# Features-first inputs and outputs, and a final norm that sums squares by products with ones

## The chip, the cores and the metric

One core of one Trainium2 chip runs the whole program. The metric is the device time of one execution in microseconds (us); lower is better. The engines are TensorE (PE in the profile, with its weight loads as PEld), VectorE (DVE), ScalarE (ACT), GpSimd (POOL) and SyncE (SP), which issues the DMAs of this kernel. Each engine runs its own instructions in order and waits on semaphores for the others.

## The reference

One layer of a streaming encoder, on a prompt of 2048 tokens and a sample of 32 (T = 2080), with 1024 features, in float32. Differential attention (group A, 4 heads of two 64-wide maps) and band attention (group B, 8 heads of 64) share one input projection and one output projection; then an MLP of 4096 with squared ReLU, a gated input embedding `p`, and a final norm:

```python
hp = hp + merge(oa, ob, subln_g[i], out_norm_b[i], w_out[i], lam_init)
hp = ffn_ple(hp, p_prompt[i], g_mlp[i], w_up[i], w_down[i], w_ple_gate[i], w_ple_proj[i])
...
y_prompt = rmsnorm(hp, g_final)

def ffn_ple(h, p, g_mlp, w_up, w_down, w_ple_gate, w_ple_proj):
    c = rmsnorm(h, g_mlp)
    h = h + jnp.square(jax.nn.relu(c @ w_up)) @ w_down
    return h + jax.nn.sigmoid(h @ w_ple_gate) * (p @ w_ple_proj)
```

Returned are `y` for prompt and sample, and the new keys and values of both groups.

## The kernel before

Features lie on the 128 partitions, tokens on the free axis, in four blocks of 512 tokens (the last has 544, worked in two slices of 272). Each product in float32 precision is made of three: both operands are split into a rounded high part and the rest (`split`: ACT makes the high part, POOL or DVE the low one), and `mm3` (lines 216 to 218) adds high x high, high x low and low x high in PSUM. Weights come through `wunit`: a load into `wr`, then the split into `wh` and `wl` (`piece` in the later stages).

The tensors in memory have tokens first, so the kernel turns blocks with TensorE, by transposes against the identity `ident`:

- `prep` (line 360) loads a tile of 128 tokens, sums its squares on ACT, turns it (`xp`, line 380), makes the activations `aH` and `aL` from PSUM with the gain, and writes the turned tile to the scratch `xT`, from which `outproj` later reads the residual `hd`.
- `knat` in `proj` turns the new keys back to tokens first (`ktp`, lines 516 and 525) for the outputs `ka_p`, `kb_p` and so on; `caches` turns the cached keys (`ctp`).
- `prep_p` turns the embedding input (`ppt`, line 907) and writes its split to the scratch `pS`, from which `gate` reads `pT`.
- `final` (line 1387) turns the finished `h` back (`yp`, line 1403), sums squares on ACT (`junk`), makes the reciprocal root for each token, multiplies with the root and the gain on DVE (line 1432) and writes rows of `y`. For block 3 the first half of the features is turned while the last gate products run (`phased`), the second half after them.

The stages follow each other: projections and attention of groups A and B, output projection `outproj`, then for each block the MLP (`mlp` for blocks 0 and 1, `mlp7` for 2 and 3), the gate and the final norm. `weave` interleaves two generators: the final of block 0 is emitted beside the MLP of block 2, that of block 2 beside the MLP of block 3, that of block 1 ahead of the output projection of block 2, and that of block 3 beside its own gate. `mlp7` computes the up products with seven instead of eight block products, with sums of weights (`s`, `wr`, lines 1255 to 1258) and of products (`u`, `r`, line 1228) on DVE and POOL; `h<-h,dps` (line 1217) adds the down products. The order on each engine is set by the tile framework's scheduler, from the order of emission and its own timeline; all DMAs go through SP's queue in that order. PSUM pools in the last part are `mm` (two banks) and `md` (six).

## Time and profile before

| | us |
|---|---|
| median of 3 runs | 3105.26 |
| lowest and highest | 3100.71, 3106.78 |
| the profiled execution | 3106.68 |
| its span in the trace | 3104.9 |
| PE busy | 2990.2 |
| POOL busy | 1852.7 |
| DVE busy | 1826.0 |
| ACT busy | 1776.4 |

In rows of groups (line, engine, operation, output<-inputs, shapes, count) the first number after the bar is the group's busy time in us, the second the mean of one in ns; after the second bar stands the idle time of the engine ahead of them and what ended it. Rows of a stretch give its bounds, its length, busy time (and count) of PE, PEld, DVE, ACT and POOL, then the granted clock, the share of the DMA engines and GB/s. Rows of a timeline give start, length, engine, line, operation and count. Rows of waits read: who waited, on whom, us in all, times, longest. A row of DMA issues gives count, KB of each and the median us from issue to landing.

### The profile page before, as it was taken

How to read it: one execution, taken by the hardware profiler on the slowest of the kernel's cores; microseconds unless marked ns; L12 is line 12 of the kernel's file. 1: busy time of each engine (PE TensorE's matmuls, PEld its weight loads, DVE VectorE, ACT ScalarE, POOL GpSimd, SP SyncE). 2: the span in 40 equal slices, each digit the busy share in tenths (PEclk: the TensorE clock that was granted, in tenths of full speed). 3: DMA queues.
4: the chain of work that ended last, by engine and by line, in shares of the span. 5: the costliest groups of instructions: out<-in, count | busy, mean ns of one | idle time of the engine just before them, and what ended most of it. 6: DMA issues, size and time to landing. Idle time of an engine off the chain costs nothing. (4 is left out here: it accounts for less than half of the span.)

```text
span 3104.9 us, 51763 instructions
## 1 busy us (share of the span) xinstructions
PE 2990.2 (96%) x17801; PEld 2637.0 (85%) x17801; DVE 1826.0 (59%) x4404; ACT 1776.4 (57%) x3434; POOL 1852.7 (60%) x2512
## 2 busy tenths in 40 slices
PE   8999989999899999999999999999899999999998
PEld 7788879899777888878888888878788887999998
DVE  6157565564565455456666656635667885576663
ACT  6256565765666666556556556554655555554545
POOL 2456746413446544556655555677878888767674
PEclk9999999999999999999999999999999999999999
DMA  9798776976877554555655454348434446333231
GB/s 283 258 263 247 224 218 187 280 221 186 247 230 226 159 155 136 154 157 167 196 152 140 124 145 139 123 150 260 155 116 130 146 158 226 118 109 102 90 117 57
DMA packets 523279, 539.19 MB, mean 174 GB/s; under 512 B 38749, under 2 KB 401569, under 8 KB 523017
## 3 DMA queue, kind: packets, MB, share of 16 engines
q1 hardware_dynamic: 523016, 535.89, 57.5%
q8 instruction: 141, 2.31, 0.3%
q14 instruction: 122, 0.99, 0.1%
HBM read 421.97 MB, written 117.75 MB: 174 GB/s over the span
## 5 line engine op out<-in xcount | busy, mean ns | idle before, releaser
L176 POOL TENSOR_TENSOR wl<-wr,wh 128x256 fp32r<-128x256 f32 x648 | 478.9, 771 | 317.8 <-ACT wh L181 277.9
L181 ACT ACTIVATE piece<-wr 128x512 fp32r<-128x512 f32 x406 | 245.4, 624 | 265.0 <-PE ups L217 111.2
L176 POOL TENSOR_TENSOR piece<-wr,piece 128x256 fp32r<-128x256 f32 x404 | 327.5, 836 | 104.6 <-ACT piece L181 85.7
L181 ACT ACTIVATE wh<-wr 128x1024 fp32r<-128x1024 f32 x228 | 240.4, 1055 | 188.1 <-PE ups L217 46.8
L166 POOL TENSOR_TENSOR wl<-wr,wh 128x256 fp32r<-128x256 f32 x264 | 201.9, 797 | 188.1 <-ACT wh L181 185.3
L216 PE MATMUL dps<-uh,piece 128*128 128x272 f32 (+1 forms) x768 | 246.3, 324 | 6.2 <-DVE h L1217 2.5
L166 POOL TENSOR_TENSOR piece<-wr,piece 128x256 fp32r<-128x256 f32 x280 | 235.1, 871 | 26.7 <-ACT piece L181 25.5
L218 PE MATMUL dps<-uh,piece 128*128 128x272 f32 (+1 forms) x768 | 246.9, 324 | 1.8 <-POOL piece L166 1.6
L217 PE MATMUL dps<-ul,piece 128*128 128x272 f32 (+1 forms) x768 | 247.3, 323 | 0.2 <-DVE ul L187 0.2
L216 PE MATMUL ups<-cs,piece 128*128 128x256 f32 (+1 forms) x864 | 245.8, 285 | 0.9 <-DVE r L1228 0.8
L217 PE MATMUL ups<-cs,piece 128*128 128x256 f32 (+1 forms) x864 | 245.7, 285 | 0.0
L218 PE MATMUL ups<-cs,piece 128*128 128x256 f32 (+1 forms) x864 | 245.5, 284 | 0.0
L216 PE MATMUL qps<-aH,wh 128*128 128x512 f32 (+1 forms) x640 | 227.9, 357 | 1.1 <-DVE ql L488 1.1
L217 PE MATMUL qps<-aL,wh 128*128 128x512 f32 (+1 forms) x640 | 228.0, 356 | 0.0
L218 PE MATMUL qps<-aH,wl 128*128 128x512 f32 (+1 forms) x640 | 227.6, 356 | 0.0
L1217 DVE TENSOR_TENSOR h<-h,dps 128x272 f32<-128x272 f32 (+1 forms) x384 | 188.9, 514 | 52.6 <-PE dps L218 51.7
L1169 DVE TENSOR_TENSOR h<-h,dps 128x512 f32<-128x512 f32 x256 | 173.3, 682 | 69.0 <-PE dps L218 67.4
L665 ACT ACTIVATE e<-e,nm 128x128 f32<-128x128 f32 (+16 forms) x136 | 157.2, 1156 | 94.9 <-DVE nm L663 92.9
L216 PE MATMUL dps<-uh,wh 128*128 128x512 f32 x512 | 207.0, 404 | 1.8 <-DVE h L1169 1.8
L216 PE MATMUL ups<-cH,wh 128*128 128x512 f32 x512 | 202.8, 397 | 1.9 <-ACT cH L181 1.9
L217 PE MATMUL ups<-cL,wh 128*128 128x512 f32 x512 | 202.5, 396 | 1.8 <-POOL cL L166 1.2
L218 PE MATMUL ups<-cH,wl 128*128 128x512 f32 x512 | 202.7, 396 | 0.0
(311 smaller groups left out, 9369.8 us busy)
## 6 DMA issues: line engine op xcount, KB each, us to landing
wr<-w_up SPq DMA_DIRECT2D x128, 512.0 KB, 4.0
wr<-w_down SPq DMA_DIRECT2D x128, 512.0 KB, 3.9
wr<-w_in SPq DMA_DIRECT2D x74, 512.0 KB, 5.5
q<-qS SPq DMA_DIRECT2D x128, 256.0 KB, 5.2
v<-vSa SPq DMA_DIRECT2D x64, 512.0 KB, 4.8
ka<-kS SPq DMA_DIRECT2D x32, 512.0 KB, 6.8
wr<-w_out SPq DMA_DIRECT2D x32, 512.0 KB, 4.6
wr<-w_ple_gate SPq DMA_DIRECT2D x32, 512.0 KB, 4.2
```

Of the source, the lines that this page charges most:

```text
L166: nc.gpsimd.tensor_tensor(out[:, sl], a[:, sl], b[:, sl], op=op)
L176: nc.gpsimd.tensor_tensor(out[:, sl], a[:, sl], b[:, sl], op=op)
L181: nc.scalar.activation(hi, raw, AF.Copy)
L216: nc.tensor.matmul(ps, lh, rh, start=start and i == 0, stop=False)
L217: nc.tensor.matmul(ps, lh, rl, start=False, stop=False)
L218: nc.tensor.matmul(ps, ll, rh, start=False, stop=stop and i == n - 1)
L665: nc.scalar.activation(row, row, AF.Exp, bias=nmx, accum_out=z[:nr, m : m + 1])
L1169: nc.vector.tensor_tensor(hv, hv, ps, op=ALU.add)
L1217: nc.vector.tensor_tensor(hv, hv, ps, op=ALU.add)
```

## The change

The host code hands `x` and `p` over a second time or only in features-first form (`x_t` and `p_t`, shape 128 x 8 x 2080 and 128 x 2 x 2080, made by `columns`), the cached keys turned (`ck_t`) and the gains as columns; `y_t` and the new keys (`ka_pt` and so on) leave features first, and numpy turns them after the launch. In the kernel:

- `prep` loads each tile twice: features first from `x_t`, multiplied with the gain on DVE and split, and tokens first from `x_prompt` for the squares alone. The scratch `xT` is gone; `outproj` reads `x_t`. The weights of the first value units get buffers of their own (`wr0`).
- `proj` writes the new keys from `kr` directly; `knat`, `prep_p` and the scratch `pS` are gone; a new `ptile` loads `p_t` and splits it at the gate.
- `final` stays features first: squares on ACT, their sum over the eight feature tiles on DVE and POOL, a split, two products with `ones` (`yss`) that sum over the partitions and spread the result, the root on ACT and DVE, and the multiplication of `h` in place, whence `y_t` is written.

```diff
@@ prep
-            x = pp.tile([P, D], F32, tag="x", name="x")
-            self.dma(x[:n], self.xsrc(t0, n))
+            xt = pp.tile([P, 8, P], F32, tag="xt", name="xt")
+            self.dma(xt[:, :, :n], self.xT[:, :, t0 : t0 + n])
...
+            x = pp.tile([P, D], F32, tag="x", name="x")
+            self.dma(x[:n], self.xsrc(t0, n))
+            m = 2 if b == 0 and i == 0 else 1
+            for k in range(0, 8, 8 // m):
+                ks = slice(k, k + 8 // m)
+                xg = xt[:, ks, :n]
+                g = self.g_attn[:, ks].unsqueeze(2).broadcast_to([P, 8 // m, n])
+                nc.vector.tensor_tensor(xg, xg, g, op=ALU.mult)
+                self.split(aH[:, ks, c0 : c0 + n], aL[:, ks, c0 : c0 + n], xg, "act", "dve")
             st = pp.tile([P, 1], F32, tag="st", name="st")
-            for h in range(2):
-                xp = mm.tile([P, 4, P], F32, tag=tag, name="xp")
-                for k in range(4):
-                    kk = 4 * h + k
-                    nc.tensor.transpose(xp[:, k, :n], x[:n, kk * P : kk * P + P], self.ident[:n, :n])
...
-            self.dma(self.xT[:, :, t0 : t0 + n], xt[:, :, :n])
+            nc.scalar.activation(x[:n], x[:n], AF.Square, accum_out=st[:n])
@@ proj
+                    if grp == 0 or b == 3:
+                        t0 = 512 * b if grp == 0 else 0
+                        self.dma(ko_p[P * g : P * g + P, t0 : t0 + 512], raw[:, :512])
+                    if b == 3:
+                        self.dma(ko_s[P * g : P * g + P], raw[:, 512 : 512 + SS])
                     yield
-                    def knat(b=b, g=g, raw=raw):
...
@@ caches
-            self.dma(kn, ck)
-            tps = tp.tile([P, 4, P], F32, tag="mm", name="ctp")
-            for g in range(4):
-                nc.tensor.transpose(tps[:, g], kn[:, P * g : P * g + P], self.ident)
+            tf = sg.tile([P, BLK], F32, tag="kr", bufs=2, name="ckr")[:, :512]
+            self.dma(tf, ck)
@@ gate
+    def ptile(self, b, up, wk):
+        n, t0 = BN[b], 512 * b
+        pT = [[up.tile([P, BLK], F32R, tag="u", name="pT") for _ in range(2)] for _ in range(2)]
+        for k in range(2):
+            raw = (
+                up.tile([P, up.aw], F32, tag="u", name="praw") if wk is None
+                else wk.tile([P, BLK], F32, tag="tmp", bufs=self.nt, name="praw")
+            )[:, :n]
+            self.dma(raw, self.pT[:, k, t0 : t0 + n])
+            self.split(pT[0][k][:, :n], pT[1][k][:, :n], raw, "act", "dve")
+        return pT
@@ final
-    def final(self, b, h, up, fk, mm, md=None):
...
+    def final(self, b, h, wk, mm):
+        nc = self.nc
+        n, t0 = BN[b], 512 * b
+        end = b == 3
+        sq = wk.tile([P, BLK], F32, tag="acc", bufs=2, name="sqy")[:, :n]
+        for k in range(8):
+            tmp = sq if k == 0 else wk.tile([P, BLK], F32, tag="tmp", bufs=self.nt, name="ysq")[:, :n]
+            for s0, sn in SUBS[b] if k == 7 else [(0, n)]:
+                sub = slice(s0, s0 + sn)
+                hv, tv, sv = h[:, k, sub], tmp[:, sub], sq[:, sub]
+                nc.scalar.activation(tv, hv, AF.Square)
+                if end and k < 7:
+                    nc.scalar.activation(hv, hv, AF.Copy, scale=self.g_final[:, k : k + 1])
+                if k > 0:
+                    if end or k % 2:
+                        nc.vector.tensor_tensor(sv, sv, tv, op=ALU.add)
+                    else:
+                        self.pool_tt(sv, sv, tv, ALU.add)
+            if end or k % 2:
+                yield
+        sh = wk.tile([P, BLK], F32R, tag="sh", bufs=1, name="sh")
+        sl = wk.tile([P, BLK], F32R, tag="sl", bufs=1, name="sl")
+        r = wk.tile([P, BLK], F32, tag="r", bufs=2, name="ry")
+        for s0, sn in SUBS[b]:
+            sub = slice(s0, s0 + sn)
+            v, y = sq[:, sub], r[:, sub]
+            self.split(sh[:, sub], sl[:, sub], v, "act", "dve")
+            ss = mm.tile([P, 512], F32, tag="mm", name="yss")[:, :sn]
+            nc.tensor.matmul(ss, self.ones, sh[:, sub], start=True, stop=False)
+            nc.tensor.matmul(ss, self.ones, sl[:, sub], start=False, stop=True)
+            nc.scalar.activation(v, ss, AF.Copy, scale=1.0 / D, bias=EPS)
+            nc.scalar.activation(y, v, AF.Ln)
+            nc.scalar.activation(y, y, AF.Exp, scale=-0.5)
+            nc.vector.scalar_tensor_tensor(v, v, -0.5, y, op0=ALU.mult, op1=ALU.mult)
+            nc.vector.tensor_tensor(v, v, y, op=ALU.mult)
+            nc.vector.scalar_tensor_tensor(y, v, 1.5, y, op0=ALU.add, op1=ALU.mult)
+            hv = h[:, 7, sub]
+            nc.vector.scalar_tensor_tensor(hv, hv, self.g_final[:, 7:8], y, op0=ALU.mult, op1=ALU.mult)
+            for k in range(6, -1, -1):
+                hv = h[:, k, sub]
+                if not end:
+                    nc.vector.scalar_tensor_tensor(hv, hv, self.g_final[:, k : k + 1], y, op0=ALU.mult, op1=ALU.mult)
+                elif k in (5, 6):
+                    self.pool_tt(hv, hv, y, ALU.mult)
                 else:
+                    nc.vector.tensor_tensor(hv, hv, y, op=ALU.mult)
+                if k % 4 == 0:
+                    self.dma(self.a["y_t"][:, k : k + 4, t0 + s0 : t0 + s0 + sn], h[:, k : k + 4, sub])
+        yield
```

The order on three engines' places follows. SP's queue at the start of the program, before (`x` is a token tile, `wr` a weight unit of the values):

```order
L157 DMA x<-x_prompt 128x1024
L157 DMA g_attn_s<-g_attn 128x8x1
L157 DMA wr<-w_in 128x4x256 x2
L157 DMA x<-x_prompt 128x1024
L157 DMA g_mlp_s<-g_mlp 128x8x1
L157 DMA g_b_s<-out_norm_b 128x4x1
L157 DMA g_sub_s<-subln_g 128x1
```

and now:

```order
L157 DMA xt<-x_t 128x8x128
L157 DMA g_attn_s<-g_attn 128x8
L157 DMA x<-x_prompt 128x1024
L157 DMA wr_142<-w_in 128x4x256
L157 DMA wr_151<-w_in 128x4x256
L157 DMA xt<-x_t 128x8x128
L157 DMA x<-x_prompt 128x1024
L157 DMA wr_178<-w_in 128x4x256
L157 DMA wr_187<-w_in 128x4x256
```

Two tiles of 512 KB now stand ahead of the first weight unit instead of one, and the small gains other than `g_attn` come behind the second pair of weights.

DVE beside the MLP of block 2, where the final of block 0 is woven in, before (`r` and `u` are sums of up products, `dps` down products, `wr` and `s` weight sums, `yn` a turned tile of `y`):

```order
L1448 TENSOR_TENSOR fst<-fst 128x1
L227 TENSOR_TENSOR rsv<-rsv,rsy 128x1
L228 TENSOR_TENSOR rsv<-rsv,rsy 128x1
L229 TENSOR_SCALAR rsv<-rsv 128x1
L231 TENSOR_TENSOR rsy<-rsy,rsv 128x1
L1432 SCALAR_TENSOR_TENSOR yn<-yn,rsy,gf 128x512 x2
L1217 TENSOR_TENSOR h<-h,dps 128x512
L1228 TENSOR_TENSOR r_26112<-t_26114,ups 128x256
```

and now (`sqy` is the sum of squares, `ry` the root):

```order
L1169 TENSOR_TENSOR r_26334<-t_26336,ups 128x256
L1369 SCALAR_TENSOR_TENSOR sqy<-sqy,ry 128x512
L1197 TENSOR_TENSOR s_26568<-wr 128x512
L1370 TENSOR_TENSOR sqy<-sqy,ry 128x512
L1169 TENSOR_TENSOR u_26365<-t_26336,ups 128x256
L1371 SCALAR_TENSOR_TENSOR ry<-sqy,ry 128x512
L1158 TENSOR_TENSOR h<-h,dps 128x512
L1373 SCALAR_TENSOR_TENSOR h<-h,g_final_s,ry 128x512
L1377 SCALAR_TENSOR_TENSOR h<-h,g_final_s,ry 128x512 x7
L1158 TENSOR_TENSOR h<-h,dps 128x512
L1198 TENSOR_TENSOR wr<-s_26568,wr 128x4x128
L1169 TENSOR_TENSOR u_26423<-u_26365,ups 128x256
```

Before, two multiplications for a token tile stood between the MLP's operations, four times in the block; now eight feature tiles are multiplied in one run. The same run stands in the MLP of block 3.

DVE at the end of the program, before (`fss` sums the squares' halves, `yo` is the second half of the features):

```order
L1384 TENSOR_TENSOR h<-h,sig 128x272
L1439 TENSOR_TENSOR fss<-fsa 128x5
L227 TENSOR_TENSOR rsv<-rsv,rsy 128x5
L228 TENSOR_TENSOR rsv<-rsv,rsy 128x5
L229 TENSOR_SCALAR rsv<-rsv 128x5
L231 TENSOR_TENSOR rsy<-rsy,rsv 128x5
L1432 SCALAR_TENSOR_TENSOR yo<-yp,rsy,gf 128x512 x4
L1432 SCALAR_TENSOR_TENSOR yo<-yp,rsy,gf 32x512
```

and now, up to the first of the two slices of 272 (the second repeats the last five rows):

```order
L1313 SCALAR_TENSOR_TENSOR sig<-gps,sig 128x272
L1351 TENSOR_TENSOR sqy<-sqy,ysq 128x272
L1328 TENSOR_TENSOR sig<-sig,pps 128x272
L187 TENSOR_TENSOR sl<-sqy,sh 128x272
L1331 TENSOR_TENSOR h<-h,sig 128x272
L1351 TENSOR_TENSOR sqy<-sqy,ysq 128x272
L187 TENSOR_TENSOR sl<-sqy,sh 128x272
L1369 SCALAR_TENSOR_TENSOR sqy<-sqy,ry 128x272
L1370 TENSOR_TENSOR sqy<-sqy,ry 128x272
L1371 SCALAR_TENSOR_TENSOR ry<-sqy,ry 128x272
L1373 SCALAR_TENSOR_TENSOR h<-h,g_final_s,ry 128x272
L1381 TENSOR_TENSOR h<-h,ry 128x272 x5
```

The root is now a row of tokens that is worked out on all partitions, once for each slice, and DVE does the six multiplications of a slice behind it; POOL does the other two.

More of the change, by code (lines that the diff above doesn't have):

```diff
@@ L190, in wunit @@
         nc = self.nc
-        raw = self.rawp.tile([P] + shape, F32, bufs=2, name="wr")
+        if pool is None:
+            raw = self.rawp.tile([P] + shape, F32, bufs=2, name="wr")
+        else:
+            raw = pool.tile([P] + shape, F32, tag="wr0", bufs=4, name="wr0")
         self.dma(raw, src)
@@ L481, in proj @@
                         )
-                        while late:
-                            late.pop(0)()
                         h_, l_ = hi[:, s0 : s0 + n], lo[:, s0 : s0 + n]
@@ L1665, in run, with columns @@
             g = self.gate(3, h, up, cs, md)
-            f = self.final(3, h, up, fk, mm, md)
-            for _ in range(5):
-                next(g)
-            for _ in range(3):
-                next(g)
-                next(f, None)
-                next(f, None)
-            drain(f)
+            f = self.final(3, h, wk, mm)
+            weave(g, f, 1)
 OUTS = {
-    "y_prompt": (1, SP, D),
-    "y_sample": (1, SS, D),
-    "ka_p": (SP, 512),
+    "y_t": (P, 8, T),
+    "ka_pt": (512, SP),
     "va_p": (SP, 512),
-    "kb_p": (512, 512),
+    "kb_pt": (512, 512),
     "vb_p": (512, 512),
-    "ka_s": (SS, 512),
+    "ka_st": (512, SS),
     "va_s": (SS, 512),
-    "kb_s": (SS, 512),
+    "kb_st": (512, SS),
     "vb_s": (SS, 512),
 }
+def columns(*parts):
+    t = np.concatenate(parts).T
+    return np.ascontiguousarray(t.reshape(-1, P, T).transpose(1, 0, 2))
 def kernel(**inputs):
     arrays = {k: np.ascontiguousarray(v) for k, v in inputs.items()}
-    for n in ("cache_a_k", "cache_a_v", "cache_b_k", "cache_b_v"):
+    for n in ("cache_a_v", "cache_b_v"):
         arrays[n] = arrays[n].reshape(PAST, 512)
+    ck = [arrays.pop(n).reshape(PAST, 4, P) for n in ("cache_a_k", "cache_b_k")]
+    arrays["ck_t"] = np.ascontiguousarray(np.stack(ck).transpose(0, 3, 2, 1)).reshape(2, P, 512)
+    arrays["x_t"] = columns(arrays["x_prompt"][0], arrays["x_sample"][0])
+    arrays["p_t"] = columns(arrays.pop("p_prompt")[0, 0], arrays.pop("p_sample")[0, 0])
+    for n in ("g_attn", "g_mlp", "out_norm_b", "subln_g", "g_final"):
+        arrays[n] = np.ascontiguousarray(arrays[n].reshape(-1, P).T)
     arrays["onehot_a"], arrays["onehot_b"] = onehots()
```

196 lines of the change are left out of this document (36 added, 160 removed).

## The prediction

> **What bounds the kernel now.** I read the page first (busy time of each engine, the 40 slices), then busy time by stretch, then the groups by line and shape, the waits, and last the two ends of the timeline.
>
> ```profile
> PE 2990.2 (96%) x17801; PEld 2637.0 (85%) x17801; DVE 1826.0 (59%) x4404; ACT 1776.4 (57%) x3434; POOL 1852.7 (60%) x2512
> PE   8999989999899999999999999999899999999998
> PEclk9999999999999999999999999999999999999999
> ```
>
> ```profile
> 80.00:100.00 20.00, 20.00 (x94) 15.50 (x93) 3.18 (x5) 2.29 (x3) 4.26 (x6) 1.00 0.78 238
> 2800.00:3000.00 200.00, 200.00 (x1601) 200.00 (x1600) 127.99 (x260) 98.45 (x170) 138.81 (x178) 1.00 0.30 96
> ```
>
> TensorE (PE) is busy 2990 of 3104.9 us, at a full granted clock, and idle for 114.7 us in all. No other engine reaches 61% (PEld is PE's own weight loads). In the two stretches it has no idle time: 94 products of 512 columns in 20 us are one each 0.213 us. So a PE instruction that goes away is worth its pitch, if what feeds PE can follow.
>
> The profiled execution took 3106.68 us, 1.8 us more than its span; the median of the three runs is 3105.26. I sum changes on the span and take them off the median.
>
> **The transposes that go.** The program loses five kinds of PE transposes against the identity: `xp` (17 token tiles x 8 = 136), `yp` (136), `ktp` (88), `ppt` (34), `ctp` (8), 402 in all. The four largest groups hold 368 of them:
>
> ```profile
> L380 PE MATMUL xp<-ident,x 128*128 128x128 f32 x128 | 20.7, 293 | 6.2 <-DMA x<-x_prompt 4.4 <-DVE kr L493 1.1 <-ACT vraw L434 0.5
> L1403 PE MATMUL yp<-ident,h 128*128 128x128 f32 x128 | 17.4, 274 | 3.8 <-ACT junk L1413 2.8 <-DVE h L1384 1.0
> L516 PE MATMUL ktp<-ident,kr 128*128 128x128 f32 x80 | 12.7, 273 | 1.8 <-ACT kn L518 1.8
> L907 PE MATMUL ppt<-ident,pn 128*128 128x128 f32 x32 | 4.9, 274 | 0.3 <-DVE ppl L911 0.3
> ```
>
> ```profile
> 2716.30 0.87 PE yp L1403 x8
> 3088.79 1.76 PE yp L1403 x16
> ```
>
> The mean of 274 ns is from start to modelled end and overlaps the next instruction. The chain of waits gives what PE is held for: 8 in 0.87 us and 16 in 1.76 us, 0.109 us each. That makes 402 x 0.109 = 43.8 us. The upper bound is the groups' busy time, 20.7 + 17.4 + 12.7 + 4.9 = 55.7 us for 368, so 60.8 us for 402: it counts each batch's pipeline end, which the following product mostly covers. I take the pitch.
>
> Not all of it is on the path. The first 16 `xp` fall where PE waits for weights anyway (below), 16 x 0.109 = 1.7 us. The last 24 `yp` come after the last gate product and belong to the tail, 2.6 us. That leaves 39.5 us.
>
> Waits that stand in front of transposes go as well: 1.1 + 0.5 (`xp`), 2.8 (`yp`), 1.8 (`ktp`), 6.2 us; the 0.3 of `ppt` I leave out, the 4.4 is the start and the 1.0 the end. The next product would find part of the same lateness (the PSUM bank of the evicting engine); I take half, 3.1 us (bounds 0 and 6.2).
>
> **What is added on PE.** Three blocks' `yss` products with ones, 6 x 0.213 = 1.3 us (the last block's four are in the tail). They stand in the order after a finished output tile, so a late sum of squares would hold PE there; the three sit beside products that do not need them, and I add nothing.
>
> **The start.** First PE products of the program, before:
>
> ```profile
> 4.41 1.94 PE L380 MATMUL xp<-ident,x 128*128 128x128 f32 x8 [4.41 <-DMA x<-x_prompt]
> 7.76 1.06 ACT L181 ACTIVATE wh<-wr 128x1024 fp32r<-128x1024 f32 x1 [1.73 <-DMA wr<-w_in]
> 8.87 0.58 PE L216 MATMUL vps<-wh,aH 128*128 128x256 f32 x1 [2.52 <-ACT wh L181]
> 8.90 5.54 POOL L176 TENSOR_TENSOR wl<-wr,wh 128x256 fp32r<-128x256 f32 x8 [7.41 <-ACT rsy L226]
> 11.34 1.91 PE L380 MATMUL xp<-ident,x 128*128 128x128 f32 x8
> 0.00:20.00 20.00, 12.16 (x64) 10.80 (x65) 10.13 (x38) 13.58 (x39) 6.47 (x15) 1.00 0.91 257
> ```
>
> PE's first real product waited for ScalarE's cast of the first weight unit, which had waited for that unit's load; POOL's eight low halves (5.54 us) then pace the next ones, and the second eight transposes fill that gap. Now a features-first tile and a token tile (512 KB each) come ahead of the weights instead of one token tile: 512 KB at that stretch's 257 GB/s is 2.0 us more. Against it, the gain vector now comes as 128 runs of 32 bytes in place of 1024 elements of 4, and the split of a tile takes three wide operations in two halves instead of eight narrow ones behind transposes. I take +1 us (bounds -1 and +3).
>
> Later loads change little: the token tiles are still read for their squares, `x_t` is read where `xT` was written (both 512-byte runs, 512 KB a tile), `pS` and its reading back go away. Nothing more is counted for them.
>
> **The final norm in the MLP.** Its vector work moves from pairs of operations per token tile to one run per block, as the order in the section on the change shows: seven multiplications that follow each other directly, eight with the one ahead. They stand in VectorE's queue (DVE) in front of the MLP's bank evictions `h<-h,dps`, the weight sums `wr` and the products `u`.
>
> ```profile
> L1432 DVE SCALAR_TENSOR_TENSOR yn<-yn,rsy,gf 128x512 f32<-128x512 f32 x24 | 24.9, 1078 | 0.4
> L1432 DVE SCALAR_TENSOR_TENSOR yo<-yp,rsy,gf 128x512 f32<-128x512 f32 x4 | 2.7, 745 | 0.1
> L1411 DVE COPY yn<-yp 128x512 f32<-128x512 f32 x24 | 15.7, 679 | 4.9 <-PE yp L1403 4.9
> PE dps L216 <- DVE h L1217: 2.5, 2, 1.8
> PE ups L216 <- DVE r L1228: 0.8, 1, 0.8
> ```
>
> Eight at 1.08 us hold DVE for 8.6 us. PE goes on in that time as long as it has banks: two in one pool and six in the other, and an output tile of six 512-column products takes 6 x 0.213 = 1.3 us, so eight banks are some 10 us. Before, two copies (1.4 us), two multiplications (2.2 us) and five small operations stood together too, and PE lost at most 1.8 us at a time to a late `h`. I take 1 us for each of the two finals that run beside an MLP, +2 us (bounds 0 and 17.2, the whole of both runs).
>
> The Trainium skill, "SBUF — State Buffer", in its account of the port pair that DVE and GpSimd share, says that a DVE operation with two SBUF inputs and a GpSimd operation that reads SBUF exclude each other for a whole instruction. The trace is in line with it: with both inputs in SBUF, in a stretch where POOL works, the multiplication takes 1078 ns, and 745 ns with one input in PSUM. The change puts more such pairs together, so by this rule the upper bound is nearer than by the banks; it is the second rival.
>
> The final of block 1 runs beside the output projection of block 2, where POOL is the nearer limit:
>
> ```profile
> 2080.00:2100.00 20.00, 18.93 (x91) 15.13 (x92) 9.94 (x16) 9.27 (x26) 14.03 (x20) 1.00 0.50 148
> 2200.00:2220.00 20.00, 14.92 (x56) 10.88 (x54) 14.55 (x18) 11.96 (x23) 18.27 (x21) 0.91 0.47 159
> L176 POOL TENSOR_TENSOR wl<-wr,wh 128x256 fp32r<-128x256 f32 x648 | 478.9, 771 | 317.8 <-ACT wh L181 277.9
> ```
>
> Six added sums of squares at 0.77 us (4.6 us) join a POOL that is 70 to 91% busy there. I take half of that block's 32 transposes as not gained, 32 x 0.109 / 2 = +1.7 us (bounds 0 and 4.6).
>
> **The tail.** After the last gate product:
>
> ```profile
> 3088.15 0.40 ACT L1362 ACTIVATE sig<-gps 128x272 f32<-128x272 f32 x1 [1.43 <-PE gps L218]
> 3088.58 0.43 ACT L1363 ACTIVATE sig<-sig 128x272 f32<-128x272 f32 x1
> 3088.63 2.46 PE L1403 MATMUL yp<-ident,h 128*32 128x128 f32 x21
> 3091.61 0.44 DVE L1384 TENSOR_TENSOR h<-h,sig 128x272 f32<-128x272 f32 x1
> 3092.11 0.55 PE L1403 MATMUL yp<-ident,h 128*128 128x128 f32 x3 [1.02 <-DVE h L1384]
> 3101.76 0.49 SPq L157 DMA_DIRECT2D y_sample<-yo  x1
> wr<-w_up SPq DMA_DIRECT2D x128, 512.0 KB, 4.0
> y_prompt<-yn SPq DMA_DIRECT2D x28, 256.0 KB, 2.1
> ```
>
> Before, from the last gate's first ScalarE step (ACT) at 3088.15 to the end are 16.75 us. Now, with a step of 272 columns at 0.46 us on ACT and 0.47 on DVE, gaps in: three ACT steps (1.4), the minimum on DVE (0.5), exponential on ACT, product, the low half of the first slice and the last add to `h` on DVE (0.47 + 3 x 0.47), square on ACT and add on DVE (0.46 + 0.47): 4.7 us. Then three steps on ACT until the first slice's exponential is done (1.4), and 2 x 9 operations on DVE, three for the root and six multiplications for each slice (18 x 0.47 = 8.5): 14.6 us. The last output of 544 KB lands 4.0 us after its issue if it goes like the 512 KB loads: 18.6 us, +1.8, say +2 (bounds: 0 with a landing as of `y_prompt`, +5 if POOL's four multiplications slow DVE's by 1078/745 and the landing is late).
>
> **The sum.** -39.5 - 3.1 + 1.3 + 1 + 2 + 1.7 + 2 = -34.6 us. From 3105.26: **3071 us**.
>
> **The rivals.**
> *Transposes cost more than their pitch* (their batches also break the stream): 60.8 in place of 43.8, on the 362 of 402 that count another 15.3 us, and all 6.2 us of waits: -34.6 - 15.3 - 3.1 = -53, 3052 us. For it speaks the busy time, against it that eight transposes between products hold PE 0.87 us.
> *DVE's runs reach PE:* both runs of eight in full, 17.2 in place of 2 us: -19.4, 3086 us. For it: behind them in DVE's queue stand evictions and weight sums. Against it: eight banks.
> *Slower: the output DMAs hold up the weights.* SP issues in order, and the two `y_t` of a final wait for DVE's run while the next `w_up` and `w_down` stand behind them.
>
> ```profile
> SPq L157 <- DVE yn L1432: 40.5, 19, 5.5
> ```
>
> If PE runs dry of weights for the run, the landing and the first low half (8.6 + 4.0 + 0.8 = 13.4 us) at each of three finals, that is 40 us, and +4 us in all, with the two DVE us already in it: 3109 us. It decides from 34.6 / 3 = 11.5 us a place. Against it: SP waited on `yn` 19 times, up to 5.5 us, and no wait of PE's comes from there.
> *The freed time is not used:* the waits of other engines (114.7 us of idle PE now) grow by what PE gains, and the time stays within 0.2%, about 6 us, which is what a measurement of this kernel can tell from none: 3104 us.
>
> **How the numbers follow.** Forecast 0.60, dearer transposes 0.15, DVE's runs 0.14, slower 0.06, not used 0.05. Faster by over 0.2%: 0.60 + 0.15 + 0.14 = 0.89; same 0.05; slower 0.06. The likeliest case's own range, from its bounds, is 3058 to 3084. The range takes in the first two rivals with their margins, 3042 to 3094, and leaves out the last two and some of the edges.
>
> **What would show it.** Right: no transpose group but `rp`, `tpp` and `tpb`; PE's instructions fewer by 392; busy PE lower by some 43 us and idle about the same 115 us; the first product at 9 to 11 us; 18 to 19 us from the last gate's first ACT step to the end. Wrong: idle PE up by 10 us or more, with waits for `h`, `r` or `piece` at the two runs of multiplications (second rival) or for loads behind `y_t` (third); or busy PE lower by about 60 us (first).

## The result, and the profile after

The changed kernel takes 3085.89 us (median of 4 runs, 3081.23 to 3090.34), the kernel before on the same chip 3102.99 us: a ratio of 0.9943, 95% interval 0.9926 to 0.9961. Run again on another chip it came to 3090.20 us, 0.9958 (0.9944 to 0.9973). By the medians it is faster by 17 and by 14 us, where the forecast was 34.6. The profiled execution has a span of 3088.5 us, 16.4 under the 3104.9 of before. Its totals, and the digits of PE's busy share and granted clock in 40 slices:

```profile
PE 2965.4 (96%) x17409; PEld 2609.3 (84%) x17409; DVE 1809.8 (59%) x4221; ACT 1751.3 (57%) x3234; POOL 1902.4 (62%) x2533
PE   6999999999899999999999999999899999999997
PEclk9999999999799999999999999999999999999999
```

392 PE instructions are gone, as the prediction counted, but busy time fell by 24.8 us instead of some 43, and idle time rose from 114.7 to 123.1. The first slice and the eleventh are the thin ones. Busy time by stretch says more, first of the kernel before:

```profile
0.00:100.00 100.00, 89.51 (x585) 78.46 (x586) 51.13 (x164) 50.01 (x140) 26.19 (x43) 1.00 0.89 275
100.00:500.00 400.00, 377.39 (x2175) 327.06 (x2174) 218.53 (x640) 226.07 (x498) 243.44 (x353) 0.98 0.79 236
500.00:1000.00 500.00, 470.96 (x2995) 422.83 (x2994) 268.34 (x885) 316.15 (x662) 209.94 (x323) 0.98 0.79 230
2000.00:3000.00 1000.00, 972.53 (x6271) 885.25 (x6270) 658.43 (x1117) 522.37 (x998) 762.01 (x933) 0.99 0.45 145
```

The same stretches of the changed kernel:

```profile
0.00:100.00 100.00, 75.51 (x473) 66.77 (x474) 49.74 (x128) 52.22 (x123) 28.55 (x37) 0.93 0.88 276
100.00:500.00 400.00, 391.29 (x2338) 344.06 (x2337) 215.17 (x564) 211.10 (x403) 275.42 (x380) 1.00 0.79 236
500.00:1000.00 500.00, 464.75 (x2756) 409.55 (x2755) 261.61 (x883) 311.75 (x647) 204.80 (x321) 0.94 0.77 224
2000.00:3000.00 1000.00, 971.83 (x6242) 885.87 (x6240) 651.24 (x1056) 524.39 (x949) 790.28 (x953) 0.99 0.44 143
```

PE does less in the first 100 us (idle 24.5 instead of 10.5), more from 100 to 500 (8.7 instead of 22.6), and less again from 500 to 1000, at a lower clock.

To put a time on each stretch I made a ledger from the start times of PE's products. Both kernels stream the same 6,162,592 columns through PE, once the transposes that go and the products with ones of the new final norm are left out. The *lead* of a kernel at a time t of the kernel before is how much earlier it has streamed as many columns. It counts the columns of any product, so work that is drawn forward raises it for a while. The forecast's own sum, laid out in the same way (76 of the 402 transposes stand in the first 100 us, then 134 to 500 us, 38 to 780, 18 to 1000, none to 2000, 96 to 3000, 40 behind; each other term at its place), stands beside it:

```
lead in us at        100    500    780   1000   1300   1400   2000   3000    end
forecast's terms     5.6   21.9   26.0   28.0   28.0   28.0   28.0   34.9   34.6
the change          -8.4   31.6   36.9   17.3   17.4   17.5   17.5   19.3   16.4
the change again   -10.9   29.3   39.5   20.2   20.4   19.7   16.2   20.1   16.5
```

Three places differ: the start (14 us under the forecast, made good by 500 us), 780 to 1000 us (20 us lost, where 2 should have been won), and all from 2000 us on (nothing won of 6.6).

**The start.** Waits of PE in the first 60 us, before (one row) and then after the change (two rows):

```profile
PE vps L216 <- ACT vraw L434: 1.0, 1, 1.0
PE vps L219 <- ACT vraw L429: 12.8, 4, 5.4
PE vps L219 <- ACT wh L181: 10.0, 1, 10.0
```

ScalarE in that stretch of the changed kernel (timeline: start, length, line, operation, idle time before it):

```profile
33.74 1.06 ACT L385 ACTIVATE x<-x 128x1024 f32<-128x1024 f32 x1 [0.85 <-DMA x<-x_prompt]
35.26 1.04 ACT L385 ACTIVATE x<-x 128x1024 f32<-128x1024 f32 x1
37.01 0.46 ACT L429 ACTIVATE vraw<-vps,rcol 128x256 f32<-128x256 f32 x1
49.19 1.06 ACT L385 ACTIVATE x<-x 128x1024 f32<-128x1024 f32 x1 [2.42 <-DMA x<-x_prompt]
50.82 1.06 ACT L385 ACTIVATE x<-x 128x1024 f32<-128x1024 f32 x1
52.76 0.47 ACT L429 ACTIVATE vraw<-vps,rcol 128x256 f32<-128x256 f32 x1
```

Twice, two squares of token tiles stand in ACT's queue in front of an eviction of the V products; the first of each pair waits for its load, and PE's next product waits for the eviction (5.3 us before 37.5, 5.4 before 53.3). One tile of each pair isn't even the start's own: the square no longer needs block 2's activation buffers, so the program's order lets block 2's token tiles run ahead into the first 70 us, where the DMA engines are busy for 97% of the time. The loads issued in that time (the start has eight tiles of each kind):

```profile
x<-x_prompt SPq DMA_DIRECT2D x13, 512.0 KB, 6.6
xt<-x_t SPq DMA_DIRECT2D x9, 512.0 KB, 7.9
```

**780 to 1000 us.** When the input projections are through, the output projection is the next work that PE can put between attention B's products. The rows below are the last projection products and the first output-projection products (first and last start at the end of the numbers), of before and then of the change:

```profile
L217 PE MATMUL qps<-aL,wh x320: 283/289/475, 529.3 to 827.4; 128*128 128x272 f32 x128, 128*128 128x512 f32 x32
L216 PE MATMUL ops<-oact,wh x128: 387/389/776, 850.1 to 980.6; 128*128 128x512 f32 x128
```

```profile
L221 PE MATMUL qps<-aH,wl x313: 282/289/476, 500.8 to 778.1; 128*128 128x272 f32 x125, 128*128 128x512 f32 x32
L219 PE MATMUL ops<-oact,wh x128: 387/389/776, 828.8 to 960.1; 128*128 128x512 f32 x128
```

The projections end 49 us earlier, the output projection begins only 21 us earlier. Between them PE has attention B alone: 22.6 us before, 50.7 us now. These are the groups of that gap in the changed kernel and then its stretch; and of the gap before the score products and the stretch:

```profile
L800 PE MATMUL sb<-kbt,q 128*128 128x320 f32 x48 | 14.7, 444 | 6.6 <-DVE stb L803 6.6
L852 PE MATMUL ob<-pb,vbt 128*128 128x512 f32 (+1 forms) x36 | 14.4, 526 | 3.7 <-DVE pb L831 3.7
L822 PE MATMUL tpb<-ident,eb 128*128 128x128 f32 x58 | 13.4, 362 | 2.5 <-DVE pb L831 2.4
778.00:828.00 50.00, 37.46 (x144) 29.11 (x143) 28.31 (x106) 33.15 (x69) 6.78 (x15) 0.66 0.70 198
```

```profile
L831 PE MATMUL sb<-kbt,q 128*128 128x320 f32 x24 | 5.8, 362 | 3.7 <-DVE stb L834 3.7
828.00:850.00 22.00, 16.21 (x85) 11.45 (x84) 14.12 (x55) 15.99 (x35) 4.34 (x8) 1.00 0.92 271
```

48 score products `sb` of attention B's heads stand in that gap; before it was 24. This is the order that the scheduler wrote: counted in the two traces, 176 score products start ahead of the last projection product now, and 204 did before. The place of the transposes was filled with projections, and not with attention's heads, whose steps on DVE and ACT follow each other. At 780 us, with as many columns streamed, the changed kernel has started 42 projection products more and 16 score products fewer; at 1000 us the counts are level but for 2 and 4. So a part of the 36.9 us at 780 us is work drawn forward, and behind it the heads' chain sets the pace alone.

### The profile page after: what moved, and what is told of

It reads as the page before. It is cut to its first block, busy times and chain, and to the rows that moved or that the text cites. A ratio compares the mean times of both kernels' runs of the same rounds, so it can differ in the third digit from the quotient of the medians.

```text
span 3088.5 us, 50476 instructions
## 1 busy us (share of the span) xinstructions
PE 2965.4 (96%) x17409; PEld 2609.3 (84%) x17409; DVE 1809.8 (59%) x4221; ACT 1751.3 (57%) x3234; POOL 1902.4 (62%) x2533
## 5 line engine op out<-in xcount | busy, mean ns | idle before, releaser
L176 POOL TENSOR_TENSOR wl<-wr,wh 128x256 fp32r<-128x256 f32 x648 | 496.0, 797 | 261.0 <-ACT wh L181 218.7
L166 POOL TENSOR_TENSOR wl<-wr,wh 128x256 fp32r<-128x256 f32 x264 | 198.4, 783 | 202.1 <-ACT wh L181 201.9
L220 PE MATMUL dps<-ul,wh 128*128 128x512 f32 x512 | 202.7, 396 | 0.0
```

The lines of the kernel that those rows point to most:

```text
L166: nc.gpsimd.tensor_tensor(out[:, sl], a[:, sl], b[:, sl], op=op)
L176: nc.gpsimd.tensor_tensor(out[:, sl], a[:, sl], b[:, sl], op=op)
L220: nc.tensor.matmul(ps, lh, rl, start=False, stop=False)
```

## The experiments

Each run is compared with the kernel before on its own chip. The ledger of all of them, with the ratio:

```
lead in us at        100    500    780   1000   1300   1400   2000   3000    end   ratio (95% interval)
late token tiles    -3.2   23.8   31.2    9.1   10.2    6.0    7.8   11.7    8.4   0.9970 (0.9955 to 0.9985)
no statistics       -0.1   40.7   46.2   27.1   27.8   25.6   24.8   29.8   27.7   0.9920 (0.9895 to 0.9945)
old start           -3.9   35.6   39.7   17.3   18.0   17.6   16.1   24.4   23.0   0.9919 (0.9895 to 0.9944)
no multiplications  -9.5   30.9   40.5   17.5   18.2   15.3   15.7   28.1   22.6   0.9952 (0.9932 to 0.9972)
first tile held     -3.7   29.2   35.1   11.5   12.4   10.3   10.0   16.8   13.7   0.9957 (0.9944 to 0.9969)
old final          -10.4   28.1   33.1   16.8   19.5   19.5   19.5   17.1   16.7   0.9938 (0.9923 to 0.9953)
old start, held      0.4   29.9   36.8   17.0   17.1   16.9   14.5   23.1   21.0   0.9939 (0.9926 to 0.9953)
norm later          -9.6   26.6   34.9   26.3   28.8   13.4    8.7   10.8    7.4   0.9969 (0.9957 to 0.9980)
before, norm later  -0.2    2.5   -1.8   -2.3   -1.0   -1.7   -2.0   -1.5   -1.4   1.0020 (1.0007 to 1.0032)
mixed                2.7   40.6   50.0   41.0   43.6   28.6   29.9   34.2   32.3   0.9905 (0.9887 to 0.9923)
mixed, q first       0.9   37.8   44.7   36.4   38.1   23.3   23.0   21.7   20.3   0.9935 (0.9919 to 0.9950)
```

Nine of the traces keep the change's order around 800 us: the change's two and the first seven kernels of this table. In all nine, 44 or 48 score products stand between projections and output projection, that gap is 45.7 to 52.4 us long, and 16 to 24 us of lead go between 780 and 1000 us, whether 31.2 or 46.2 us come in. So the place takes about a fixed amount; it does not bring every kernel to one level.

### Block 2's token tiles held back by a buffer

```diff
-            x = pp.tile([P, D], F32, tag="x", name="x")
-            self.dma(x[:n], self.xsrc(t0, n))
+            if b < 2:
+                x = pp.tile([P, D], F32, tag="x", name="x")
+                self.dma(x[:n], self.xsrc(t0, n))
...
+            if b > 1:
+                x = pp.tile([P, 8, P], F32, tag="xt", name="x").rearrange("p a b -> p (a b)")
+                self.dma(x[:n], self.xsrc(t0, n))
             st = pp.tile([P, 1], F32, tag="st", name="st")
             nc.scalar.activation(x[:n], x[:n], AF.Square, accum_out=st[:n])
```

> Blocks 2 and 3 only: the token tile of the statistics is loaded into the features-first tile's own buffer, after its split, so neither its load nor its square can run ahead of block 2's activations; the start's own tiles are as in the change. Theory 1 (token tiles of block 2 run ahead into the start, take load time there and stand with their squares in ScalarE's queue in front of the V evictions): TensorE's idle time in the first 100 us falls from 24.5 to 10 to 14 us, waits of V products for vraw in the first 60 us from 12.8 to under 3 us, the granted clock in 30 to 60 us is 1.00 again, and the time is 3069 to 3076 us, 0.989 to 0.991 of the kernel before. Theory 2 (the new preparation of blocks 0 and 1 itself costs it: two tiles to load and wide steps on ScalarE and VectorE for each): 3083 to 3088 us, idle time in the first 100 us over 20 us. Theory 3 (the gain is lost later, in attention at a lower clock): idle time may fall at the start, the time stays 3080 to 3088 us.

3095.03 us, 0.9970. The start is better as theory 1 said, but only by a third of what it asked: 20.2 us idle in the first 100, 7.1 us of waits for `vraw`. And the time is worse than the change's: none of the three theories has it there. The ledger shows where: beside the change, 8 us of lead are missing at 500 us and 6 at 780. I put that down to the serial buffer, which makes block 2's preparation late; no run isolates it. Theory 1 explains a part of the start and nothing of the time.

### No statistics at all

```diff
+        nc.vector.memset(self.rcol, 1.0)
...
-            x = pp.tile([P, D], F32, tag="x", name="x")
-            self.dma(x[:n], self.xsrc(t0, n))
...
-            st = pp.tile([P, 1], F32, tag="st", name="st")
-            nc.scalar.activation(x[:n], x[:n], AF.Square, accum_out=st[:n])
             r = self.rcol[:n, 4 * b + i : 4 * b + i + 1]
-            self.rsqrt(pp, st[:n], 1, 1.0 / D, EPS, nc.vector, "r1", n, out=r)
```

> Leaves out the tokens' statistics in all blocks: no token tile, square or root, every token's factor is one. Theory 1: what this saves over the run with late token tiles is small, 0 to 4 us, so 3066 to 3074 us. Theory 2: the price of the start's token tiles shows, 3060 to 3070 us here while the run with late token tiles stays above 3083. Theory 3: 3078 to 3086 us.

3078.87 us, 0.9920: in theory 3's range, and above those of the other two. Without token tiles the start loses 8 to 11 us less than in the change, and this lead lives: 46.2 us at 780. Yet 19 us go between 780 and 1000 here too, over a gap of 49.3 us between projections and output projection; what is left at 1000 us, 27.1, is still 7 to 10 us above the change's two executions.

### The start as before

```diff
-                gen = (y for b in HALVES[0] for y in self.prep(b, acts, pp, ring, "s", first if b == 0 else None))
+                gen = (y for b in HALVES[0] for y in self.prep_old(b, acts, pp, ring, "s", first if b == 0 else None))
```

> The preparation of blocks 0 and 1 as before (one token tile, transposes, and the write of the transposed copy, to a scratch array that nothing reads); blocks 2 and 3 and all the rest as in the change. Theory 1: block 2's token tiles can still run ahead, so the start stays disturbed: idle time of TensorE in the first 100 us 14 to 25 us, 3080 to 3090 us. Theory 2: the start is as before, idle time some 11 us, 3072 to 3078 us (the sum's 3071 plus 48 transposes of 0.109 us that are back, less the 1 us of the start). Theory 3: as theory 2 at the start, the time 3084 to 3092 us.

3078.37 us, 0.9919: at theory 2's upper edge, with idle time of 15.7 us, which is theory 1's. By the idle time both causes are at work at the start. But at 780 us the lead (39.7) is that of the change run again (39.5): the better start had been evened out by then, and the 7 us that this run is ahead at the end came after 2000 us.

### No multiplications in two finals

```diff
+            if b not in (0, 2):
-            nc.vector.scalar_tensor_tensor(hv, hv, self.g_final[:, 7:8], y, op0=ALU.mult, op1=ALU.mult)
+                nc.vector.scalar_tensor_tensor(hv, hv, self.g_final[:, 7:8], y, op0=ALU.mult, op1=ALU.mult)
```

(the other seven in the same way)

> Leaves out the eight multiplications of the final norm in blocks 0 and 2, the two finals beside an MLP; their sums, products with ones and roots stay. If the runs of multiplications cost the 2 us that the forecast gave them or less, 3083 to 3087 us. If they reach TensorE in full (the second rival of the prediction), 3068 to 3074 us.

3087.97 us, 0.9952: no faster than the change. The interval leaves out the second rival of the prediction, VectorE's runs reaching TensorE in full, whose 3068 us to 3074 us would be a ratio of 0.988 to 0.990. Whether the runs cost the 2 us of the forecast or some more stays open: the profiled execution, the fastest of this kernel's five at 3084.1 us, gained 12 us of lead from 2000 to 3000 us, the change's 2 to 4, and lost 5.5 of it again to the end.

### The change again, and block 2's first token tile held

> The changed kernel itself, unaltered, as the measure for the runs beside it: 0.993 to 0.996 of the kernel before, TensorE idle for some 24 us in the first 100 us. All theories expect the same.

3090.20 us, 0.9958, as expected. The two executions of one program show how little the split of PE's time in busy and idle means by itself: the spans are 3088.5 and 3088.3 us, busy 2965.4 and 2955.8, idle 123.1 and 132.5.

The held tile:

```diff
             x = pp.tile([P, D], F32, tag="x", name="x")
+            if b == 2 and i == 0:
+                late1 = self.rb[1][:, 0:1]
+                self.pool_tt(x[:, 0:1], late1, late1, ALU.add)
             self.dma(x[:n], self.xsrc(t0, n))
```

> Block 2's first token tile alone is held: a column of its buffer is written from block 1's row factors before the load, so the load and the square of block 2's token tiles come after the start's own; from there on all is as in the change. If the tiles that ran ahead cost what the run with late token tiles showed at the start (idle time of the first 100 us 20.2 instead of 24.5 us) and that run lost the rest later by its serial buffer, then idle time in the first 100 us is 19 to 21 us here and the time 3 to 6 us under the change. Rival: what runs ahead is work that must be done anyway, and is paid later: the time within 2 us of the change.

Its first 100 us:

```profile
0.00:100.00 100.00, 78.74 (x493) 68.45 (x494) 53.44 (x121) 49.38 (x109) 34.84 (x44) 0.95 0.90 274
```

3091.17 us, 0.9957: the rival is right. The start is better (21.3 us idle, 7 us more lead at 100 us than the change beside it), and at 500 us the two are level, 29.2 and 29.3. What had run ahead was work that is due anyway.

### The final norm as before

```diff
-            drain(self.final(1, h, wk, mm))
+            drain(self.final(1, h, uq, fk, mm))
```

(and the other three, with the old `final`, its gain row and its outputs)

> The final norm as before (transposes, token tiles out, the gain as a row), all else as in the change. By the terms of the forecast the new final is worth 112 x 0.109 = 12.2 us and 1.4 us of waits less 1.3, 2, 1.7 and 2: this run would be 6 to 7 us slower than the change. If the new finals bring next to nothing because VectorE and GpSimd pace their stretch, it is within 2.5 us of the change, either way.

3087.23 us, 0.9938, beside 3090.20 (0.9958) for the change on the same chip. The intervals overlap, so it is no slower, where the forecast's terms asked for 6 to 7 us: 126 more PE instructions cost nothing that the times show. From 2000 us to the end the old final loses 2.8 us of lead, the new one 1.1 or gains 0.3.

### The old start, held

> Blocks 0 and 1 prepared as before (token tile, transposes, and the write of the transposed copy to a scratch array that nothing reads), and block 2's first token tile held as above; the rest as in the change. If both causes at the start are real and add up, idle time in the first 100 us is 10 to 13 us (15.7 in the run with the old start alone) and the time 0.989 to 0.991 of the kernel before, 10 to 14 us under the change. If the tiles ahead are only paid later, 0.991 to 0.993 like the old start alone.

3085.74 us, 0.9939. The stretch of its start:

```profile
0.00:100.00 100.00, 87.52 (x574) 77.29 (x575) 54.50 (x176) 54.51 (x154) 27.83 (x45) 0.98 0.88 274
```

The start is right (12.5 us idle, lead 0.4) and 11 us ahead of the change beside it, as both causes together ask. At 500 us the lead is 29.9 us; the change, from -10.9, has 29.3. That isn't yet the loss made good: this run has the 64 transposes of blocks 0 and 1 back, 7.0 us at 0.109. The held tile alone, with no transpose more, was level with the change at 500 us as well; the run without statistics kept its 9 to 11 us, but it leaves out steps on ACT and DVE all through. What a start without the loss would be worth stays open between these. It isn't where the forecast goes wrong: at 500 us the change is ahead of the forecast's terms, in columns.

### Block 1's attention norm later

The output projection of block 0 needs block 0's attention outputs alone. Their loads stand behind those of block 1's norm, which wait for attention B's last head of blocks 0 and 1. This takes that order away:

```diff
-            weave2(proj_a(), [self.onorm(b, wq, mm, "mm", self.rB) for b in HALVES[0]], ONP)
+            weave2(proj_a(), [self.onorm(0, wq, mm, "mm", self.rB)], ONP)
...
             drain(self.oload(0, wq, actq, oa))
+            drain(self.onorm(1, wq, mm, "mm", self.rB))
```

> The change, with one step moved: the attention norm of block 1 (its sums of squares and its factors) comes behind the loading of block 0's attention outputs instead of ahead of it. In the changed kernel TensorE has no product but attention's own from the last projection product at 778 us to the first output-projection product at 829 us, 50.6 us, at half clock for 34; before it was 827 to 850, 22.4 us. Theory 4 (TensorE's lead of some 35 to 40 us at 780 us is given back there, because the output projection stands behind block 1's norm, which needs attention's last head): the gap shrinks to under 25 us, the granted clock in 780 to 820 us is 0.9 or more, and the time is 3066 to 3076 us, 0.988 to 0.991 of the kernel before. Rival 5 (attention's heads set the time of the whole stretch to 1300 us, so products used up earlier are missing later): the gap shrinks, the time stays 3083 to 3090 us.

3097.32 us, 0.9969. The place was right: the gap shrank from 50.7 to 2.8 us, and at 1300 us the lead is 28.8 us instead of 17 to 20. The price wasn't. Waits of PE from 1250 to 1420 us, the first load and the first score product of attention A, and two stretches:

```profile
PE s L619 <- DMA q<-qS: 14.0, 1, 14.0
PE tpp L678 <- DVE e L640: 4.1, 2, 3.7
1284.34 0.69 SPq L157 DMA_DIRECT2D ba<-dba  x1
1299.27 4.93 PE L619 MATMUL s<-ka,q 128*128 128x512 f32 x16 [14.02 <-DMA q<-qS]
1280.00:1300.00 20.00, 5.99 (x25) 4.55 (x25) 0.36 (x2) 4.12 (x8) 7.36 (x12) 0.76 0.80 186
1300.00:1320.00 20.00, 15.74 (x71) 13.34 (x70) 14.99 (x43) 12.88 (x24) 2.92 (x4) 0.81 0.73 179
```

Where attention A takes over from B, its loads go out from 1284.3 us, behind B's last product at 1282.1 us, and PE comes to the first score product at 1285.3 and stands there for 14.0 us, with MLP products behind it in its queue (3.3 us in the change). 15.4 us of lead go there, and 4.7 more to 2000 us. It isn't rival 5 as I wrote it, a stretch paced by heads all through, but its outcome: the lead is given back at another place, where the order has attention's first product next and its loads have only just gone out.

### The same step in the kernel before

> The kernel before, with the same step moved. Theory 4: the gap there is 22.4 us and lies at full clock but for 3.4 us, so there is less to win: 3095 to 3101 us, 0.997 to 0.999. If the moved step wins as much here as in the change, the two effects have nothing to do with each other and theory 4 is wrong: 3085 to 3091 us. Rival 5: 3103 to 3106 us.

3111.19 us, 1.0020 (1.0007 to 1.0032), with a gap of 5.0 us instead of 22.6. It is slower, so theory 4's figure falls here too; closing the gap by this one step alone is worth nothing in either kernel.

### A mixed kernel, and q first

The start as before (without the write of the turned tile), the final as before, block 1's norm later; all else as in the change.

```diff
-                gen = (y for b in HALVES[0] for y in self.prep(b, acts, pp, ring, "s", first if b == 0 else None))
+                gen = (y for b in HALVES[0] for y in self.prep_old(b, acts, pp, ring, "s", first if b == 0 else None))
...
+            drain(self.onorm(1, wq, mm, "mm", self.rB))
...
-            f = self.final(2, h, wk, mm)
+            f = self.final(2, h, up, fk, mm)
```

> What the runs so far favour, put together: blocks 0 and 1 prepared as before (without the write of the transposed copy, which nothing reads any more), the final norm as before, block 1's attention norm later as above; the rest as in the change. If the start, the finals and the gap add up: 3062 to 3072 us, 0.987 to 0.990. If the gap's cure already holds what a better start could bring: as the change with the norm moved, within 3 us.

3076.81 us, 0.9905 (0.9887 to 0.9923), before 3106.40 us beside it: the lowest ratio of the study, just above the 0.987 to 0.990 of its sum and far from the moved norm alone (0.9969). The lead is 50.0 us at 780, 41.0 at 1000, and again 15 us go at attention's change to A, in one wait of 13.7 us for `q`. What is left behind it, 28.6 us at 1400, is 11 us above the run with the old start (17.6), so here the closed gap does keep something. This kernel has 190 of the 402 transposes back and gains 30 us by the medians: so something other than the count of PE's instructions, the order of the work I take it, weighs more than those 190. The last run gave that place another order of loads:

```diff
+                q0 = pool.tile([P, 2, 2, 256], F32R, tag="q", bufs=2, name="q")
+                self.load_q(q0, g, (0, 1), js[0])
...
-            for hl in range(2):
...
+            for i, kt in enumerate(kts):
...
+                for hl in range(2):
```

> The mixed kernel with the order of loads changed at one place: when attention A begins its second half, the first pair's q is loaded ahead of the keys, and the first key tile's two halves ahead of the second tile's. In the mixed kernel TensorE waited there once for 13.7 us for q, and lost most of the 10 us that closing the gap at 780 us had won. If the loads' order makes that wait (theory 6: attention's change from B to A is the next place that gives the lead back): the wait falls to 4 to 9 us and the time to 3066 to 3073 us, 0.987 to 0.9895 of the kernel before. Rival 7 (the wait moves from q to the keys or to the values, all of which are loaded in the same 14 us): the same 12 to 15 us of wait under another name, and 0.990 to 0.992.

3085.26 us, 0.9935. Waits of PE from 1240 to 1420 us:

```profile
PE s L674 <- DMA ka<-kS: 10.6, 1, 10.6
PE tpp L733 <- DVE e L695: 5.7, 2, 5.5
```

Rival 7 is right about the place, not about the size: the wait goes by the name of the keys with 10.6 us, and of `e` behind them, and 14.8 us of lead are lost as before; the ratio lies above both figures. That this kernel is slower than the mixed one, and than rival 7's figure, comes mostly from other places (5 us less at 780, 6 between 2000 and 2100), whose order the scheduler made anew.

## Why the prediction was right and wrong

The direction, the count of instructions, and the range (3042 to 3094) held; the forecast of 3071 us was 15 us too fast, and the gain half of what was said. 3086 us is outside the likeliest case's own range, 3058 to 3084, but that range does not come out of its bounds: added up, they give 3060 to 3097. 3086 us is the figure of the second rival, but by chance: its mechanism fell.

- **Transposes at their pitch.** As far as 780 us the lead is more than the sum's, 36.9 us where its terms make 26.0, a part of it work drawn forward. From 100 to 500 us PE's idle time fell by 13.9 us and the clock rose from 0.98 to 1.00, beside 14.6 us of transposes. That points to waits in front of them that weighed more than the half that I took; no run separates them.
- **The step that failed** is in the first part: "a PE instruction that goes away is worth its pitch, if what feeds PE can follow". I tested that on two stretches without idle time and applied it to 362 of the 402, also to stretches where PE has idle time because attention B is all that is left. There, from 780 to 1000 us, 19.6 us were given back, so that at 1000 us the lead is 17 to 20 us where the terms make 28.0. "The freed time is not used" was the nearest rival; I gave it 0.05 because I priced it as all or nothing, and looked for it in the total of idle time. It took half of the lead, and showed as idle time only in part. Three runs close that gap to 2.8 us, and all three lose 15 us at attention A's beginning instead, with 28.8, 38.1 or 43.6 us coming in. So it isn't one wait, and it isn't a levelling: the order that the scheduler writes without the transposes has places at which PE's next product waits for attention, and each takes its amount. That the order and not the chain as such decides is what the mixed kernel speaks for; no run fixed the order and took the transposes alone away.
- **The start.** The first product came at 10.01 us (9 to 11 were said), but "Later loads change little" was wrong at its place: 8.4 us late at 100 us instead of 5.6 early. Token tiles and their squares, block 2's among them, stand in front of V's evictions. What that costs in the end stays between nothing (the held tile, level with the change at 500 us) and the 7 to 10 us that the run without statistics keeps at 1000 us.
- **The finals beside the MLPs.** The terms made 6.9 us of gain from 2000 to 3000 us; the two executions of the change show 1.8 and 3.9, and the old final in its place was no slower in time. DVE's multiplications of 512 columns, at a median of 1.22 us, are somewhat dearer than the 1.08 taken for them. This is the other part of the shortfall, and what took it is open. POOL is busy for 790.3 us of that stretch instead of 762.0. DVE's runs of eight as such cost nothing that the times show.
- **The tail.** 18 to 19 us were said from the last gate's first ACT step; it is 19.5, from 3068.97 to the end at 3088.5. The multiplications are what is longer: beside POOL's two, DVE's six of a slice take 3.5 us instead of 2.8, with five at 0.59 us in the first slice and one of 1.10 in the second:

```profile
3068.97 0.40 ACT L1309 ACTIVATE sig<-gps 128x272 f32<-128x272 f32 x1 [0.94 <-PE gps L221]
3076.16 2.97 DVE L1381 TENSOR_TENSOR h<-h,ry 128x272 f32<-128x272 f32 x5
3080.46 1.10 DVE L1373 SCALAR_TENSOR_TENSOR h<-h,g_final_s,ry 128x272 f32<-128x272 f32 x1
3077.80 6.48 SPq L157 DMA_DIRECT2D y_t<-h  x4
```

- **Loads held up by `y_t`** (the slower rival) do not show: no wait of PE's from 2000 us on is for a load itself, and those for ACT's split of a weight piece are as before (5.5 and 2.9 us, before 5.2 and 2.3).

What stays open: how much of the differences from 2000 us on, 2 to 9 us of lead between kernels whose code there is the same, is the order that the scheduler happens to choose. No run fixed that order.

## What to carry to other kernels

Price a removed instruction by the stretch it stands in: here half of the lead went at a place where a dependent chain was all that the order left to PE. So look ahead for the next place at which the filler runs out, and expect the scheduler to write another order once the instruction is gone. A lead ledger (the same work done how much earlier, by time) shows in one table where a gain is made and lost, which totals of busy and idle time hide. And when an edit takes a dependency away, look which later blocks' loads may now run ahead, and in which in-order queue they stand.

## What was not expected of the hardware

The granted clock fell to 0.66 over 778 to 828 us, although no idle time of PE was longer than 3.3 us, and the fall began behind gaps of 0.6 to 0.9 us. The timeline there:

```profile
781.71 0.97 PE L800 MATMUL sb<-kbt,q 128*128 128x320 f32 x4 [0.59 <-DVE stb L803]
783.53 0.86 PE L822 MATMUL tpb<-ident,eb 128*128 128x128 f32 x5 [0.85 <-DVE pb L831]
784.99 1.44 PE L800 MATMUL sb<-kbt,q 128*128 128x320 f32 x4 [0.59 <-DVE stb L803]
798.57 2.29 PE L852 MATMUL ob<-pb,vbt 128*128 128x512 f32 x5 [3.28 <-DVE pb L831]
```

The four score products take 1.44 us instead of 0.97 from 785 us on. The Trainium skill, "TensorE: Matmul & The Clock Gate", section "Why this matters for your kernels", asks for no idle gaps over about 3 us between bursts, after which the clock halves. The trace departs from that as a sufficient rule: gaps of under 1 us were enough, while in the kernel before the same products, with PE idle for as large a share (5.8 of 22 us, here 12.5 of 50), ran at 1.00 from 828 to 850 us. In the second execution of the changed kernel the clock held through such gaps and fell only at 794.7 us, within a wait of 5.25 us. The same page's section "A second HAM failure mode: psum-queue depth-cycling" tells of a clock that goes up and down because PE idles briefly and often between groups of products; that is nearer to what this trace shows. What decides between the two executions, no run here shows.

And as far as two executions tell, the clock wasn't what the time hung on there. The same stretch in the other execution of the changed kernel:

```profile
778.00:828.00 50.00, 33.03 (x139) 24.73 (x138) 29.83 (x107) 33.44 (x72) 6.13 (x14) 0.80 0.72 200
```

At a clock of 0.80 instead of 0.66 PE did 139 products in those 50 us, not more than the 144, and the gap, with 48 score products in it, was 50.7 us in both. PE was busy for 33.0 us of the stretch instead of 37.5: the slower products took up time in which PE would else have waited for DVE and ACT. That is how a wait can stand in the profile as busy time.
